# One more seven-product unit in the first down group of both FFNs, and the rotation tables and causal mask moved into a tile of the mixer

## The chip, the cores and the metric

The kernel runs on one core of a Trainium2 chip. Its time is the device time of one execution, in microseconds (us); several executions are timed and their median is compared. Five engines work side by side, each through its own list of instructions: PE (TensorE, the matmuls; PEld is its loading of weights), DVE (VectorE), ACT (ScalarE), POOL (GpSimd) and SP (SyncE, which only issues transfers here). They wait for each other by semaphores.

## The reference

One decoder layer on 256 rows of 2048 floats: a half-step SwiGLU FFN, a token mixer, a second FFN of the same kind, each added to the scaled stream and layer-normalised. Cut to what matters here:

```python
def swiglu(x, w_gate, w_up, w_down):            # w_gate, w_up: 2048 x 5632; w_down: 5632 x 2048
    return (jax.nn.silu(x @ w_gate) * (x @ w_up)) @ w_down
...
x = layer_norm(DEEPNORM_ALPHA * x + FFN_RES_WEIGHT * swiglu(x, ffn1_w_gate[l], ffn1_w_up[l], ffn1_w_down[l]), ...)
...
mix = jnp.concatenate([o_mla, o_nsa], axis=-1) @ w_out[l]     # the mixer: two attentions behind x @ w_in[l]
x = layer_norm(DEEPNORM_ALPHA * x + mix, ln2_g[l], ln2_b[l])
x = layer_norm(DEEPNORM_ALPHA * x + FFN_RES_WEIGHT * swiglu(x, ffn2_w_gate[l], ffn2_w_up[l], ffn2_w_down[l]), ...)
...
def rope(x, pos):                                          # the rotation: tables of cos and sin by position
    ...
    return jnp.concatenate([x1 * cos - x2 * sin, x2 * cos + x1 * sin], axis=-1)
```

Only the mixer uses the rotation tables and the causal mask.

## The kernel before

**Precision.** Everything is float32, done by split products. `split` writes `hi`, the value rounded to the matmul's type, on ACT (L95), and `lo`, what is left, on DVE (L96). `mm3` (L100 to L102) makes one product of three matmuls: hi by hi, hi by lo, lo by hi. Names in the profile: `raw` is a loaded weight tile, `whi` and `wlo` its parts; `thi` and `tlo` are the parts of the transposed activations; `sum` is a sum of weights; `m` is a 4 KB tile of the mixer's pool, of which there are `NM`.

**A stage of an FFN** (`gemm2`) computes two column chunks of 512 for both row tiles of 128. It goes through k in units of two k-tiles of 128. A plain unit has 8 products, so 24 matmuls of 128x512, and two weight tiles of 128x1024 to split. A unit in the list `seven` has 7 products, 21 matmuls, after the scheme of Strassen and Winograd: DVE adds weight tiles (L326 128x1024, L327 and L328 128x512), the sums are split too, and the products p1, p5, p6, p7 go into banks of their own. It also needs four sums of the activations (L405 to L408, 128x128), split into one `m` tile. After the last seven-product unit of a stage ACT copies p1 (L365) and DVE combines the four (L366 to L369); at the end of the stage four adds (L384) give the results. An up stage then multiplies by the gate (L516), a gate stage applies Silu on ACT (L494).

**The order of an FFN** is gate(0), up(0), gate(2), up(2), gate(4), down(0), up(4), gate(6), up(6), gate(8), up(8), the last pair `_gu`, down(1). The number is the first column chunk. The first down group, down(0), is called group one here: it multiplies what the first four chunks of the hidden layer give, eight units of k (0 to 7), into the columns of the output, first column pair cp 0, then cp 1. Both pairs take the order and the seven-product units of the table `DOWN, DOWN7`. The transposes of a hidden chunk (`trans`, L476) are spawned after its up stage and come into the next gate stage behind its last seven-product unit, at its tail: chunks 2 and 3 in gate(4)'s tail, chunks 4 and 5 in gate(6)'s... each chunk holds two units, so unit 4 is the first half of chunk 2. For a chunk with a unit in `SUMMED` the transposed bank is also copied to a `w` tile by ACT (L483), and L405 to L408 run on the copies; for the others there are only the split's cast (L485) and subtraction (L486). The banks of group one are seeded with the scaled residual by ACT (L544).

**What sets the order.** PE and SP run in the order of the program text; a small table of lanes (`tick`, `spawn`, `held`) interleaves the transposes there. On DVE, ACT and POOL a scheduler places the instructions when the program is built, and each engine then runs its list from top to bottom. Weight tiles come from rotating buffers: 5 for `raw`, 3 for `sum`, 6 each for `whi` and `wlo`.

**The constants.** `load_consts` loads 926 floats per partition into a tile `pack` in ffn1's first stage, 768 of them the rotation tables, and POOL builds the causal mask `cmask`. Both stay for the whole kernel.

Of the kernel before, what the change touches and what calls it, by code (L numbers as in the profile page):

```python
# [11 lines left out]
F32 = mybir.dt.float32  # L12
F32R = mybir.dt.float32r
AF = mybir.ActivationFunctionType
OP = mybir.AluOpType
# [3 lines left out]
P = 128  # L19
D = 2048  # L20
S = 256
NT = S // P
# [6 lines left out]
NEG = -1e30  # L29
# [4 lines left out]
O_CKV, O_KR, O_Q, O_KC, O_KS, O_KW, O_G = 512, 768, 832, 1856, 2368, 2880, 3392  # L34
KT = 2
HEAD, SPARE = 8, 2
NM = 8
NW = 9

GATE, GATE7 = (0, 1, 2, 3, 4, 5, 6, 7), (2, 4, 5)  # L40
UP, UP7 = (0, 1, 3, 2, 4, 6, 5, 7), (1, 2, 4, 5)
LATE = (0, 3, 1, 6, 2, 4, 5, 7)
DOWN, DOWN7 = (4, 0, 1, 5, 2, 3, 6, 7), (0, 1, 2, 3)
SUMMED = (0, 1, 2, 3, 8, 9, 10, 11, 18, 19, 20)
REST7 = ((8, 9, 10, 11, 18, 19, 20), (8, 9, 10, 11, 18, 19))
REST = ((12, 13, 14, 15, 8, 9, 16, 10, 11, 17, 18, 19, 20, 21), (12, 13, 8, 9, 14, 10, 11, 15, 18, 19, 16, 17, 20, 21))

# [6 lines left out]
def layer(ctx: ExitStack, tc: tile.TileContext, a: dict, out: bass.AP):  # L54
    nc = tc.nc
    PE, V, A, G = nc.tensor, nc.vector, nc.scalar, nc.gpsimd

    const = ctx.enter_context(tc.tile_pool(name="const", bufs=1))
# [17 lines left out]
    def am(dt=F32):  # L76
        return att.tile([P, 8, P], dt, name="m", bufs=NM)

# [35 lines left out]
    def spawn(gen, lane=None):  # L114

        lanes.setdefault(lane if lane is not None else object(), []).append([now[0], gen])
# [274 lines left out]
    def sl(pair, j):  # L391
        return pair[0][:, j, :], pair[1][:, j, :]
# [8 lines left out]
    def sums(v):  # L401

        x11, x12, x21, x22 = v
        s = wk([P, 4, P])
        V.tensor_tensor(s[:, 0], x21, x22, op=OP.subtract)  # L405
        V.tensor_tensor(s[:, 1], s[:, 0], x11, op=OP.subtract)
        V.tensor_tensor(s[:, 2], x11, x21, op=OP.subtract)
        V.tensor_tensor(s[:, 3], s[:, 1], x12, op=OP.add)  # L408
        return s

    def parts(s):
        hl = am2(F32R)
        split(*hl, s)
        return hl
# [3 lines left out]
    def load_x(k, n=2):  # L418
# [10 lines left out]
        if k // KT in UP7:  # L429
            xs0[k // KT] = parts(sums([raw[:, j, t * P:(t + 1) * P] for t in range(NT) for j in range(2)]))  # L430

    def load_consts():
        c = {}
        kept = sum(w for n, w in _PACK if n[:2] != "w2")
        pack = const.tile([P, kept], F32, name="pack")
        nc.sync.dma_start(pack, a["pack"][:, :kept])
        at = 0
        for n, w in _PACK:
            c[n] = (a["pack"] if n[:2] == "w2" else pack)[:, at:at + w]
            if n[:3] in ("cos", "sin"):  # L440
                c[n] = c[n].rearrange("p (t d) -> p t d", t=NT)
            at += w
        z = const.tile([P, S], F32, name="cmask")
        G.memset(z, 0.0)

        G.affine_select(out=z[:, P:], in_=z[:, P:], pattern=[[-1, P]], compare_op=OP.is_ge, fill=NEG, base=0,
                        channel_multiplier=1)
        c["mask"] = z
        one = const.tile([P, NT, NCMP], F32, name="vmask")
        G.memset(one, 1.0)  # L450
        zero = const.tile([P, NT, NCMP], F32, name="nmask")
        G.memset(zero, 0.0)
        for m, fill in ((one, 0.0), (zero, NEG)):
            G.affine_select(out=m, in_=m, pattern=[[P, NT], [-CS, NCMP]], compare_op=OP.is_ge, fill=fill,
                            base=-(CB - 1), channel_multiplier=1)
        c["valid"], c["neg"] = one, zero
        mh = const.tile([P, 1], F32, name="mhalf")
        G.memset(mh, -0.5)
        c["mhalf"] = mh
        return c  # L460


    def ffn(name, x, xs, done, begin=None, after=None, late=()):
# [3 lines left out]
        def trans(cs, ready, want=()):  # L467

            for c in cs:
                v, units = [], [i for i in range(KT) if 2 * c + i in want]  # L470
                while held[0] or now[0] < ready:
                    yield 1
                pts = [new_bank().rearrange("p (a b) -> p a b", a=4) for _ in range(NT)]
                for t in range(NT):
                    for j in range(4):
                        PE.matmul(pts[t][:, j, :], hs[c, t][:, j * P:(j + 1) * P], ident, start=j == 0, stop=j == 3,  # L476
                                  is_transpose=True, skip_group_check=True)
                for t in range(NT):
                    hT[c, t] = new_T()
                    src = pts[t]  # L480
                    if units:
                        src = wk([P, 4, P])
                        A.copy(src, pts[t])  # L483
                        v.append(src)
                    A.copy(hT[c, t][0], pts[t])  # L485
                    V.tensor_tensor(hT[c, t][1], src, f(hT[c, t][0]), op=OP.subtract)  # L486
                if units:
                    for i in units:
                        hS[2 * c + i] = parts(sums([u[:, KT * i + j] for u in v for j in range(KT)]))
                yield 2  # L490
# [22 lines left out]
        def up(c0):  # L513
# [5 lines left out]
            if c0 < 8:  # L519
                spawn(trans((c0, c0 + 1), now[0] + DFF, SUMMED), "T")  # L520

        def last():
# [8 lines left out]
            gemm2(x, xs, GATE, GATE7, name + "_gu", 0, fin)  # L531
            spawn(trans((8, 9, 10), now[0] + DLAST, SUMMED), "T")

        def down(gi):
            xh = lambda k, t: sl(hT[k // 4, t], k % 4)

            def rows(t, n):
                return y[t][:, n * NCH:(n + 1) * NCH]

            for cp in range(2):  # L540
                order, sevens = (REST[cp], REST7[cp]) if gi else (DOWN, DOWN7)
                gemm2(xh, hS, order, sevens, name + "_w_down", cp, lambda t, j, r: done(t, 2 * cp + j) if gi else None,
                      tail=3 if gi and cp else 0, into=lambda t, j: rows(t, 2 * cp + j),
                      seed=lambda t, j, b: A.activation(b, rows(t, 2 * cp + j), AF.Identity, scale=1.0 if gi else 2 * ALPHA))  # L544


        for step, n in ((gate, 0), (up, 0), (gate, 2), (up, 2), (gate, 4), (down, 0), (up, 4), (gate, 6), (up, 6), (gate, 8),
                        (up, 8)):
            step(n)
        last()  # L550
        down(1)


# [83 lines left out]
    cst = {}  # L637
# [475 lines left out]
def _rope_tables(d):  # L1113
# [7 lines left out]
_PACK = (("cos128", 256), ("sin128", 256), ("cos64", 128), ("sin64", 128), ("ln1_g", 16), ("ln1_b", 16), ("ln2_g", 16),  # L1121
         ("ln2_b", 16), ("nsa_gate_b", 24), ("mla_q_norm_g", 4), ("mla_kv_norm_g", 2), ("pe_k", 32), ("pe_v", 32), ("w2_k", 256), ("w2_v", 256))
# [69 lines left out]
```

## Time and profile before

| what | us |
|---|---|
| median of 3 runs | 1754.5 (1754.39 to 1756.76) |
| the profiled execution | 1758.64 |
| its span, first to last instruction | 1756.9 |
| PE busy (8040 matmuls) | 1736.7, 99% |
| DVE busy | 1586.5, 90% |
| ACT busy | 1023.5, 58% |
| POOL busy | 17.0, 1% |
| DMA queue of SP, share of 16 engines | 58.4% |

The profiled execution lies 4.1 us above the median, 1.7 us of which is outside the span. In ffn1 the stages that matter lie, by the trace, so (us from the start): gate(4) about 178 to 219.5, group one cp 0 219.5 to 260.3, cp 1 260.3 to 301.1, up(4) 301.1 to 341.9, gate(6) 341.9 to about 385, up(6) to 426, then gate(8). In ffn2 group one lies at 1267.2 to 1348.8 and up(6) ends at 1474. A view by stretches gives the busy time of each engine in a stretch and the granted clock; in a timeline a row gives start, duration, engine, line, operation and, in brackets, the idle time ahead of it with what ended it. Matmul durations overlap: the pitch from start to start is what counts.

### The profile page before, as it was taken

What the parts mean: (1) busy time and instruction counts of PE and PEld (TensorE: products, weight loads), DVE (VectorE), ACT (ScalarE), POOL (GpSimd) and SP (SyncE); (2) the same over time, 40 slices, a digit from 0 to 9 for tenths busy, and PEclk for the clock granted to TensorE, in tenths of its full rate; (3) what the DMA queues carried; (4) which work ended last, traced back from release to release, by engine and by line L of the source; (5) the groups of instructions that cost most, each with busy time, mean ns of one, the idle gap of its engine ahead of it and who ended that gap; (6) DMA issues with size and microseconds to landing.
All of it is one profiled execution on the core that took longest, in us unless ns stands there. A gap on an engine that the chain in (4) does not pass through costs nothing. (4 is left out here: it accounts for less than half of the span.)

```text
span 1756.9 us, 22430 instructions
## 1 busy us (share of the span) xinstructions
PE 1736.7 (99%) x8040; PEld 1428.9 (81%) x8040; DVE 1586.5 (90%) x2099; ACT 1023.5 (58%) x1354; POOL 17.0 (1%) x39
## 2 busy tenths in 40 slices
PE   9999999999999999999999999999999999999997
PEld 7888888888888887887788788888888888888886
DVE  7899999999999998865586679899999999999998
ACT  6656565565656665654365545665655565656652
POOL 0000000000000000000000001000000000000000
PEclk9999999999999999999999999999999999999999
DMA  9665656556666566546753345654656655665665
GB/s 337 218 216 172 212 198 215 185 188 200 212 206 220 168 203 232 178 159 213 260 193 131 120 169 175 216 196 168 215 192 215 205 195 200 206 201 192 204 203 180
DMA packets 100336, 350.01 MB, mean 199 GB/s; under 512 B 11136, under 2 KB 13696, under 8 KB 100224
## 3 DMA queue, kind: packets, MB, share of 16 engines
q1 hardware_dynamic: 98944, 344.39, 58.4%
q0 software_dynamic: 1280, 4.20, 0.9%
q8 instruction: 63, 1.03, 0.2%
q14 instruction: 49, 0.40, 0.1%
HBM read 346.44 MB, written 2.10 MB: 198 GB/s over the span
## 5 line engine op out<-in xcount | busy, mean ns | idle before, releaser
L100 PE MATMUL bank<-whi,thi 128*128 128x512 f32 (+1 forms) x1904 | 748.6, 393 | 1.5 <-ACT whi L95 1.5
L101 PE MATMUL bank<-wlo,thi 128*128 128x512 f32 (+1 forms) x1904 | 740.8, 389 | 3.2 <-DVE wlo L96 3.1
L102 PE MATMUL bank<-whi,tlo 128*128 128x512 f32 (+1 forms) x1904 | 740.0, 389 | 0.2 <-DVE tlo L96 0.2
L95 ACT CAST whi<-raw 128x1024 fp32r<-128x1024 f32 (+1 forms) x577 | 540.6, 962 | 270.5 <-PE bank L102 142.9
L96 DVE TENSOR_TENSOR wlo<-raw,whi 128x1024 fp32r<-128x1024 f32 (+1 forms) x577 | 631.6, 1109 | 61.0 <-ACT whi L95 60.1
L95 ACT CAST whi<-sum 128x1024 fp32r<-128x1024 f32 x271 | 282.5, 1050 | 337.8 <-DVE sum L328 124.3
L100 PEld LDWEIGHTS bank<-whi,thi 128*128 128x128 f32 x1904 | 357.9, 188 | 79.3 <-issue 4.1
L101 PEld LDWEIGHTS bank<-wlo,thi 128*128 128x128 f32 x1904 | 358.1, 188 | 77.5 <-DVE wlo L96 7.0
L102 PEld LDWEIGHTS bank<-whi,tlo 128*128 128x128 f32 x1904 | 357.8, 188 | 74.3 <-DVE tlo L96 0.6
L96 DVE TENSOR_TENSOR wlo<-sum,whi 128x1024 fp32r<-128x1024 f32 x271 | 324.9, 1216 | 32.4 <-ACT whi L95 29.9
L100 PE MATMUL bank<-whi,m 128*128 128x512 f32 x448 | 174.3, 389 | 0.0
L101 PE MATMUL bank<-wlo,m 128*128 128x512 f32 x448 | 174.3, 389 | 0.0
L102 PE MATMUL bank<-whi,m 128*128 128x512 f32 x448 | 174.3, 389 | 0.0
L326 DVE TENSOR_TENSOR sum<-raw 128x1024 f32<-128x1024 f32 x112 | 136.7, 1220 | 12.4 <-DMA raw<-in_ffn_w_up 10.5
L101 PEld LDWEIGHTS bank<-wlo,m 128*128 128x128 f32 x448 | 84.1, 188 | 17.5
L102 PEld LDWEIGHTS bank<-whi,m 128*128 128x128 f32 x448 | 84.1, 188 | 17.5
L100 PEld LDWEIGHTS bank<-whi,m 128*128 128x128 f32 x448 | 84.1, 188 | 17.5
L328 DVE TENSOR_TENSOR sum<-sum,raw 128x512 f32<-128x512 f32 x112 | 76.9, 686 | 0.2
L327 DVE TENSOR_TENSOR sum<-sum,raw 128x512 f32<-128x512 f32 x112 | 76.8, 686 | 0.1
L384 DVE TENSOR_TENSOR w<-bank,w 128x512 f32<-128x512 f32 x80 | 51.8, 683 | 2.2 <-PE bank L102 2.2
L777 ACT ACTIVATE w<-w,mx 128x256 f32<-128x256 f32 (+1 forms) x48 | 21.3, 445 | 27.5 <-DVE mx L773 24.6
L384 DVE TENSOR_TENSOR y<-bank,w 128x512 f32<-128x512 f32 x32 | 20.7, 683 | 6.8 <-PE bank L102 6.8
(187 smaller groups left out, 946.5 us busy)
## 6 DMA issues: line engine op xcount, KB each, us to landing
raw<-in_ffn_w_down SPq DMA_DIRECT2D x176, 512.0 KB, 4.5
raw<-in_ffn_w_up SPq DMA_DIRECT2D x160, 512.0 KB, 4.7
raw<-in_ffn_w_gate SPq DMA_DIRECT2D x146, 512.0 KB, 4.7
raw<-in_ffn_gu SPq DMA_DIRECT2D x32, 512.0 KB, 5.0
raw<-in_w_in SPq DMA_DIRECT2D x30, 512.0 KB, 5.2
raw<-in_w_out SPq DMA_DIRECT2D x20, 512.0 KB, 3.3
sum<-in_w_in SPq DMA_DIRECT2D x18, 512.0 KB, 5.3
sum<-in_ffn_w_gate SPq DMA_DIRECT2D x12, 512.0 KB, 4.8
```

The source lines that it names most:

```text
L95: A.copy(hi, src)
L96: V.tensor_tensor(lo, src, f(hi), op=OP.subtract)
L100: PE.matmul(ps, xh, wh, start=first and not onto, stop=False, skip_group_check=onto)
L101: PE.matmul(ps, xh, wl, start=False, stop=False, skip_group_check=onto)
L102: PE.matmul(ps, xl, wh, start=False, stop=last, skip_group_check=onto)
L326: V.tensor_tensor(t13, a_, b_[:, 1:2, :].broadcast_to([P, 2, NCH]), op=OP.add)
L327: V.tensor_tensor(t24[:, 0], t13[:, 0], a_[:, 1], op=OP.add)
L328: V.tensor_tensor(t24[:, 1], t24[:, 0], b_[:, 0], op=OP.add)
L384: V.tensor_tensor(r, B[b], rest[b], op=OP.add)
L777: A.activation(s[:, h, :], s[:, h, :], AF.Exp, bias=mx[:, h:h + 1], accum_out=sm[:, h:h + 1])
```

## The change

The table for group one now has one entry for each column pair. cp 0 keeps its order and its four seven-product units. cp 1 takes the units in the order 5, 0, 1, 6, 2, 3, 4, 7, and 0 to 4 are seven-product units: five, the last three of them in a row. Unit 4 joins `SUMMED`, so chunk 2's transposes get the two copies, the four sums and a split into one more `m` tile, in gate(4)'s tail of both FFNs. `NM` goes from 8 to 9. To make room, the rotation tables (768 floats per partition) and the mask leave the constants; after ffn1 a fresh `m` tile takes both, by one transfer and two POOL instructions.

```diff
--- before.py
+++ after.py
@@ -34,14 +34,14 @@
 O_CKV, O_KR, O_Q, O_KC, O_KS, O_KW, O_G = 512, 768, 832, 1856, 2368, 2880, 3392
 KT = 2
 HEAD, SPARE = 8, 2
-NM = 8
+NM = 9
 NW = 9
 
 GATE, GATE7 = (0, 1, 2, 3, 4, 5, 6, 7), (2, 4, 5)
 UP, UP7 = (0, 1, 3, 2, 4, 6, 5, 7), (1, 2, 4, 5)
 LATE = (0, 3, 1, 6, 2, 4, 5, 7)
-DOWN, DOWN7 = (4, 0, 1, 5, 2, 3, 6, 7), (0, 1, 2, 3)
-SUMMED = (0, 1, 2, 3, 8, 9, 10, 11, 18, 19, 20)
+DOWN, DOWN7 = ((4, 0, 1, 5, 2, 3, 6, 7), (5, 0, 1, 6, 2, 3, 4, 7)), ((0, 1, 2, 3), (0, 1, 2, 3, 4))
+SUMMED = (0, 1, 2, 3, 4, 8, 9, 10, 11, 18, 19, 20)
 REST7 = ((8, 9, 10, 11, 18, 19, 20), (8, 9, 10, 11, 18, 19))
 REST = ((12, 13, 14, 15, 8, 9, 16, 10, 11, 17, 18, 19, 20, 21), (12, 13, 8, 9, 14, 10, 11, 15, 18, 19, 16, 17, 20, 21))
 
@@ -429,23 +429,18 @@
         if k // KT in UP7:
             xs0[k // KT] = parts(sums([raw[:, j, t * P:(t + 1) * P] for t in range(NT) for j in range(2)]))
 
+    TAB = sum(w for n, w in _PACK if n[:3] in ("cos", "sin"))
+
     def load_consts():
         c = {}
-        kept = sum(w for n, w in _PACK if n[:2] != "w2")
+        kept = sum(w for n, w in _PACK if n[:2] != "w2") - TAB
         pack = const.tile([P, kept], F32, name="pack")
-        nc.sync.dma_start(pack, a["pack"][:, :kept])
+        nc.sync.dma_start(pack, a["pack"][:, TAB:TAB + kept])
         at = 0
         for n, w in _PACK:
-            c[n] = (a["pack"] if n[:2] == "w2" else pack)[:, at:at + w]
-            if n[:3] in ("cos", "sin"):
-                c[n] = c[n].rearrange("p (t d) -> p t d", t=NT)
+            if at >= TAB:
+                c[n] = a["pack"][:, at:at + w] if n[:2] == "w2" else pack[:, at - TAB:at - TAB + w]
             at += w
-        z = const.tile([P, S], F32, name="cmask")
-        G.memset(z, 0.0)
-
-        G.affine_select(out=z[:, P:], in_=z[:, P:], pattern=[[-1, P]], compare_op=OP.is_ge, fill=NEG, base=0,
-                        channel_multiplier=1)
-        c["mask"] = z
         one = const.tile([P, NT, NCMP], F32, name="vmask")
         G.memset(one, 1.0)
         zero = const.tile([P, NT, NCMP], F32, name="nmask")
@@ -538,7 +533,7 @@
                 return y[t][:, n * NCH:(n + 1) * NCH]
 
             for cp in range(2):
-                order, sevens = (REST[cp], REST7[cp]) if gi else (DOWN, DOWN7)
+                order, sevens = (REST[cp], REST7[cp]) if gi else (DOWN[cp], DOWN7[cp])
                 gemm2(xh, hS, order, sevens, name + "_w_down", cp, lambda t, j, r: done(t, 2 * cp + j) if gi else None,
                       tail=3 if gi and cp else 0, into=lambda t, j: rows(t, 2 * cp + j),
                       seed=lambda t, j, b: A.activation(b, rows(t, 2 * cp + j), AF.Identity, scale=1.0 if gi else 2 * ALPHA))
@@ -658,6 +653,20 @@
 
     ffn("ffn1", lambda k, t: sl(xT[k // 4, t], k % 4), xs0, done1, begin=begin, after=load_y)
 
+
+    tab = am().rearrange("p a b -> p (a b)")
+    nc.sync.dma_start(tab[:, :TAB], a["pack"][:, :TAB])
+    at = 0
+    for n, w in _PACK:
+        if at < TAB:
+            cst[n] = tab[:, at:at + w].rearrange("p (t d) -> p t d", t=NT)
+        at += w
+    z = tab[:, TAB:TAB + S]
+    G.memset(z, 0.0)
+
+    G.affine_select(out=z[:, P:], in_=z[:, P:], pattern=[[-1, P]], compare_op=OP.is_ge, fill=NEG, base=0,
+                    channel_multiplier=1)
+    cst["mask"] = z
 
     w_in = W["w_in"]
     xin = lambda k, t: sl(x1[k // 4, t], k % 4)
```

Line numbers shift with it: L483, L485, L486, L494, L516 and L544 of before are L478, L480, L481, L489, L511 and L539 of the changed kernel.

On PE six matmuls are gone in the whole program (7840 to 7834 rows of its list), three in each cp 1 of group one; nothing else moves there. On SP the early transfer of `pack` is 128x158 in place of 128x926, and a transfer `m<-in_pack 128x768` stands behind ffn1's last weight loads and ahead of the mixer's first. On POOL the mask's two instructions stand in the same place. DVE and ACT get the added instructions, and the scheduler orders them otherwise in both FFNs, from gate(4)'s tail to up(4) and again from gate(6)'s tail to gate(8); the mixer's order is the same.

First place: ACT in gate(4)'s tail and at the start of group one. `L365` is gate(4)'s copy of p1, `whi<-raw` are casts of weight tiles, `L485`/`L480` the casts of transposed chunks, `L544`/`L539` the seeds. Before:

```order
L365 COPY w<-bank 128x512
L95 CAST whi<-raw 128x1024 x5
L485 CAST thi<-bank 128x512 x2
L95 CAST whi<-raw 128x1024
L95 CAST whi<-raw 128x512
L95 CAST whi<-sum 128x1024
L485 CAST thi<-bank 128x512 x2
```

Now:

```order
L365 COPY w<-bank 128x512
L95 CAST whi<-raw 128x1024 x6
L478 COPY w<-bank 128x512
L480 CAST thi<-bank 128x512
L478 COPY w<-bank 128x512
L480 CAST thi<-bank 128x512
L95 CAST whi<-raw 128x512
L95 CAST m<-w 128x512
```

The sixth weight cast, which is that of group one's first seven-product unit, stood behind chunk 2's casts and now stands ahead of them and of the two new copies. On DVE one weight split and then chunk 2's `tlo` stand behind L369 in this place.

Second place: ACT in gate(6)'s tail, the transposes of chunks 4 and 5. Before:

```order
L365 COPY w<-bank 128x512
L95 CAST whi<-raw 128x1024 x5
L483 COPY w<-bank 128x512
L485 CAST thi<-bank 128x512
L483 COPY w<-bank 128x512
```

Now:

```order
L365 COPY w<-bank 128x512
L95 CAST whi<-raw 128x1024 x6
L478 COPY w<-bank 128x512
L480 CAST thi<-bank 128x512
L478 COPY w<-bank 128x512
```

Here too one weight cast more stands ahead of the copies.

Third place: DVE from up(6)'s last seven-product unit to gate(8). `wlo<-sum` are the two splits of the sums of that unit; the `wlo<-raw` behind them are the two tiles of up(6)'s last, plain unit and then gate(8)'s first tiles. Before:

```order
L96 TENSOR_TENSOR wlo<-sum,whi 128x1024 x2
L96 TENSOR_TENSOR wlo<-raw,whi 128x1024 x2
L366 TENSOR_TENSOR w<-bank,w 128x512
L96 TENSOR_TENSOR wlo<-raw,whi 128x1024
L367 TENSOR_TENSOR w<-bank,w 128x512
L96 TENSOR_TENSOR wlo<-raw,whi 128x1024
L368 TENSOR_TENSOR w<-bank,w 128x512
L369 TENSOR_TENSOR w<-bank,w 128x512
L384 TENSOR_TENSOR w<-bank,w 128x512 x2
L516 TENSOR_TENSOR w<-w 128x512 x2
L384 TENSOR_TENSOR w<-bank,w 128x512 x2
L516 TENSOR_TENSOR w<-w 128x512 x2
```

Now:

```order
L96 TENSOR_TENSOR wlo<-sum,whi 128x1024 x2
L96 TENSOR_TENSOR wlo<-raw,whi 128x1024
L366 TENSOR_TENSOR w<-bank,w 128x512
L96 TENSOR_TENSOR wlo<-raw,whi 128x1024
L367 TENSOR_TENSOR w<-bank,w 128x512
L96 TENSOR_TENSOR wlo<-raw,whi 128x1024
L368 TENSOR_TENSOR w<-bank,w 128x512
L369 TENSOR_TENSOR w<-bank,w 128x512
L384 TENSOR_TENSOR w<-bank,w 128x512 x2
L511 TENSOR_TENSOR w<-w 128x512 x2
L384 TENSOR_TENSOR w<-bank,w 128x512 x2
L511 TENSOR_TENSOR w<-w 128x512 x2
```

Before, four weight splits stand between the sums and the block of L384 and L516: both tiles of up(6)'s last unit and both of gate(8)'s first. Now there are three: the second tile of gate(8)'s first unit stands behind the block.

## The prediction

> **What bounds the kernel now.** I read the page's busy shares first, then the view by stretches over the FFNs, then timelines of DVE and PE at the tightest places, then the waits.
>
> ```profile
> PE 1736.7 (99%) x8040; PEld 1428.9 (81%) x8040; DVE 1586.5 (90%) x2099; ACT 1023.5 (58%) x1354; POOL 17.0 (1%) x39
> ...
> 301.10:341.90 40.80, 40.80 (x181) 33.78 (x180) 37.60 (x42) 23.47 (x25) 0.00 (x0) 1.00 0.60 198
> 170.00:426.00 256.00, 255.82 (x1146) 211.84 (x1145) 250.04 (x298) 155.18 (x182) 0.00 (x0) 1.00 0.61 203
> 1348.80:1389.60 40.80, 40.80 (x182) 33.78 (x181) 36.80 (x42) 23.33 (x25) 0.00 (x0) 1.00 0.57 191
> 1218.00:1474.00 256.00, 256.00 (x1147) 212.32 (x1146) 249.58 (x299) 154.41 (x182) 0.00 (x0) 1.00 0.60 203
> ```
>
> Columns from the second row on: the stretch, its length, busy time of PE, PEld, DVE, ACT, POOL, then the granted clock and DMA. PE is full, so matmuls removed should count at once. But from gate(4) to the end of up(6) DVE is nearly full too: 250.04 of 256 us in ffn1, so it idles 5.96 us, 3.2 of them in up(4) (301.10 to 341.90); in ffn2 6.4 and 4.0. So there are two bounds side by side, and the change takes from one and gives to the other. How little DVE is ahead shows at the end of up(6), whose last seven-product unit starts this timeline of DVE; the second fence is PE's.
>
> ```profile
> 412.24 1.24 DVE L326 TENSOR_TENSOR sum<-raw 128x1024 f32<-128x1024 f32 x1
> 413.38 1.24 DVE L96 TENSOR_TENSOR wlo<-raw,whi 128x1024 fp32r<-128x1024 f32 x1
> 414.51 0.71 DVE L327 TENSOR_TENSOR sum<-sum,raw 128x512 f32<-128x512 f32 x1
> 415.11 0.70 DVE L96 TENSOR_TENSOR wlo<-raw,whi 128x512 fp32r<-128x512 f32 x1
> 415.72 0.70 DVE L328 TENSOR_TENSOR sum<-sum,raw 128x512 f32<-128x512 f32 x1
> 416.32 2.53 DVE L96 TENSOR_TENSOR wlo<-sum,whi 128x1024 fp32r<-128x1024 f32 x2
> 419.05 2.36 DVE L96 TENSOR_TENSOR wlo<-raw,whi 128x1024 fp32r<-128x1024 f32 x2 [0.20 <-ACT whi L95]
> 421.33 0.68 DVE L366 TENSOR_TENSOR w<-bank,w 128x512 f32<-128x512 f32 x1
> ...
> 425.99 1.28 DVE L384 TENSOR_TENSOR w<-bank,w 128x512 f32<-128x512 f32 x2
> ...
> 430.79 2.35 DVE L96 TENSOR_TENSOR wlo<-raw,whi 128x1024 fp32r<-128x1024 f32 x2
> ```
>
> ```profile
> 418.05 0.39 PE L101 MATMUL bank<-wlo,m 128*128 128x512 f32 x1
> 418.28 0.39 PE L102 MATMUL bank<-whi,m 128*128 128x512 f32 x1
> ...
> 428.93 0.39 PE L101 MATMUL bank<-wlo,thi 128*128 128x512 f32 x1
> ...
> 431.43 0.39 PE L100 MATMUL bank<-whi,thi 128*128 128x512 f32 x1
> 432.06 0.50 PE L101 MATMUL bank<-wlo,thi 128*128 128x512 f32 x1 [0.25 <-DVE wlo L96]
> ```
>
> The first sum's `wlo` is done at 416.32 + 1.22 = 417.54 and PE uses it at 418.05: DVE is 0.51 us ahead. At 431.43 it is behind: PE's next start comes after 0.63 us in place of 0.23, so 0.40 us are lost. ffn2's last up(6) unit reads alike:
>
> ```profile
> 1463.69 2.50 DVE L96 TENSOR_TENSOR wlo<-sum,whi 128x1024 fp32r<-128x1024 f32 x2
> ...
> 1465.72 0.39 PE L101 MATMUL bank<-wlo,m 128*128 128x512 f32 x1
> ```
>
> Done at 1464.91, used at 1465.72: 0.81 us ahead.
>
> **The matmuls removed.** PE's pitch is 0.23 us (418.05 to 418.28; 0.227 over many). Three matmuls less in each FFN are 0.68 us, in both 1.36 us. This counts only where PE does not wait for DVE.
>
> **What DVE is given.** Pitches are differences of starts above: 1.14 for a 128x1024 (412.24 to 413.38), 0.60 for a 128x512 (414.51 to 415.11). A seven-product unit costs L326 1.14, split 1.14, L327 0.60, split 0.60, L328 0.60 and two splits of sums 2.28, together 6.36. A plain unit costs two splits, 2.28. So unit 4 costs 4.08 more. Its activations cost four sums and one split:
>
> ```profile
> 388.06 0.29 DVE L405 TENSOR_TENSOR w<-w 128x128 f32<-128x128 f32 x1
> 388.26 0.29 DVE L408 TENSOR_TENSOR w<-w 128x128 f32<-128x128 f32 x1
> ```
>
> 4 x 0.20 + 0.60 (a 128x512 as above) = 1.40. So DVE gets 5.5 us more work in each FFN, ahead of up(6), with 0.51 us (0.81) in hand at its end. In group one itself, the third seven-product unit in a row takes DVE 6.36 us where PE needs 21 x 0.227 = 4.77, so the lead that DVE has there shrinks by 1.6 us per unit and PE begins to wait in cp 1 already; where it waits matters less than how much of the 5.5 us DVE gets back before up(6) ends. What it can get back is its idle time:
>
> ```profile
> DVE sum L326 <- DMA raw<-in_ffn_w_up: 2.9, 3, 2.0
> DVE sum L326 <- DMA raw<-in_ffn_w_down: 0.8, 1, 0.8
> ```
>
> These waits (total, times, longest) between 170 and 440 us are 3.7 of the 5.96 us. Up(4)'s 3.2 us can be won, since a DVE that is late no longer runs ahead of its loads there. The bounds are thus: nothing won, and 3.2 (ffn1) won.
>
> **What the new order on ACT takes back.** Here the row by row reading of the changed lists comes in. In gate(4)'s tail the cast of group one's first unit now stands ahead of chunk 2's copies.
>
> ```profile
> 210.21 1.08 ACT L485 CAST thi<-bank 128x512 fp32r<-128x512 f32 x2
> 212.51 1.06 ACT L95 CAST whi<-raw 128x1024 fp32r<-128x1024 f32 x1 [1.22 <-DVE tlo L486]
> ...
> 210.58 0.68 DVE L369 TENSOR_TENSOR w<-bank,w 128x512 f32<-128x512 f32 x1
> ...
> 206.62 0.33 SPq L322 DMA_DIRECT2D raw<-in_ffn_w_down  x1
> ...
> raw<-in_ffn_w_down SPq DMA_DIRECT2D x1, 512.0 KB, 5.8
> ```
>
> That cast's weights are issued at 206.62 and land 5.8 us later, at 212.4; the cast starts at 212.51 and not sooner. Before, the transposed chunk's casts were done by then (from 210.21). Now the copy starts at 212.5 + 0.95 = 213.4, its `thi` at 213.9, and DVE's `tlo` can start at 214.5. DVE, with one weight split behind L369, is free at 210.58 + 0.60 + 1.14 = 212.3: it idles 2.2 us. The second place is gate(6)'s tail:
>
> ```profile
> 374.81 1.05 ACT L95 CAST whi<-raw 128x1024 fp32r<-128x1024 f32 x1 [2.39 <-DMA raw<-in_ffn_w_up]
> 376.17 1.05 ACT L95 CAST whi<-raw 128x1024 fp32r<-128x1024 f32 x1 [0.31 <-DMA raw<-in_ffn_w_up]
> 377.12 0.58 ACT L483 COPY w<-bank 128x512 f32<-128x512 f32 x1
> ```
>
> The casts ahead of the copies wait for their loads, 1.36 us apart; with one cast more the copies come at least one such step later, and DVE, again with one weight split in hand, waits for them: I put 1.4 to 2 us. Between cp 0 and cp 1 the 0.8 us for the load of w_down stays and may double, as its buffer is freed by DVE itself. So 2.2 + 1.4 to 2 + 0.8 to 2 = 4.4 to 6.2 us of idle time stand in the new order, against 5.96 in the old: what up(4) gives back, the tails take. Of the difference, -0.2 to 1.6, I take 0.5 us won in each FFN, below its middle, as the new order will have small waits that I do not count. DVE is then 5.5 - 0.5 = 5.0 us later at up(6)'s last seven-product unit, and PE 5.0 - 0.51 = 4.5 us (ffn1) and 5.0 - 0.81 = 4.2 us (ffn2). The matmuls saved are in this already: PE would be there earlier and waits for the same DVE. Bounds: 5.0 and 4.7 with nothing won; with up(4)'s idle won in full 5.5 - 3.2 - 0.51 = 1.8 and, with 4.0 us in ffn2, 0.7.
>
> **Gate(8)'s first unit.** The order of the third place decides it. PE stands at the last unit's first sum (the 418.05 row), waiting for `wlo`. From its end DVE has to do, in the new order: the second sum's split, three splits, L366 to L369, four L384, four L516, and then the second tile of gate(8)'s first unit: 4 x 1.14 + 4 x 0.60 + 8 x 0.60 + 1.22 = 13.0 us (the block alone is 425.99 to 430.79, 4.80). PE comes to that tile 428.93 - 418.05 = 10.9 us after the first sum. It waits 13.0 - 10.9 = 2.1 us. In the old order this tile is split ahead of the block, and the tile behind it waits only 0.40; with PE 2.1 later that wait is gone, 0.40 counted once, for ffn1. If DVE kept its old lead of 0.51 or 0.81 the wait would be 1.6 or 1.3: these are the lower bounds. In both FFNs: 2 x 2.1 - 0.4 = +3.8 (bounds 2.5 to 3.8).
>
> **The tables and the mask.** The transfer is 128 x 768 x 4 bytes, 0.39 MB, at the mixer's start, ahead of w_in's loads.
>
> ```profile
> 677.00:698.00 21.00, 19.32 (x76) 14.98 (x75) 15.53 (x23) 7.27 (x11) 0.55 (x1) 0.92 0.87 305
> ...
> 694.39 0.69 DVE L384 TENSOR_TENSOR y<-bank,w 128x512 f32<-128x512 f32 x1 [2.91 <-PE bank L102]
> 697.23 1.52 ACT L608 ACTIVATE y<-y,mr,rstd 128x512 f32<-128x512 f32 x2 [8.05 <-DVE mr L603]
> ```
>
> At 305 GB/s it takes 1.3 us and the DMA engines are 0.87 busy, so w_in's first tiles land up to 1.3 us later. Their splits lie ahead of DVE's wait of 2.91 us and ACT's of 8.05, which hide it. I take 0; without that cover it costs 1.3. The tile's last reader was done in `_gu`, so SP does not stop at it, and nothing behind it queues. POOL's two instructions lie beside a POOL that is busy 1%. The lighter first transfer frees time where PE is not waiting for it: 0.
>
> **Sum.** 4.5 + 4.2 + 3.8 = +12.5 us. The profiled execution would go from 1758.64 to 1771.1; it lies 4.1 above the median, so the median goes from 1754.5 to about 1767.
>
> **Rivals.**
> (a) As above: 1767, its own range 1763 to 1770. Chance 0.60.
> (b) Up(4)'s idle time is won in full, so the tails' new idle costs nothing: 1.8 + 0.7 + 3.8 = +6.3, so 1761. For it: a load's wait shifts with DVE; against it: 212.4 is a landing, not DVE's doing. Chance 0.18.
> (c) Not slower: DVE's lead covers all. It would need DVE over 2.1 us ahead at up(6)'s last seven-product unit in spite of 5.5 us more work; then PE's six matmuls count, -1.36, so 1753.1. It decides from the point where the lead at 418.05 falls under 2.1 us; the trace has 0.51 there with less work. For it speaks only that DVE may wait less on ACT and loads than the old rows show. Chance 0.10.
> (d) The clock falls after a wait.
>
> ```profile
> 685.00:688.40 3.40, 1.72 (x6) 0.91 (x6) 1.80 (x4) 2.55 (x4) 0.00 (x0) 1.00 0.77 275
> 688.40:691.80 3.40, 3.40 (x10) 2.62 (x9) 3.08 (x6) 0.78 (x2) 0.00 (x0) 0.50 0.98 363
> ```
>
> After 3.4 us in which PE was busy 1.72, the granted clock was 0.50 for 3.4 us, which costs 1.7. A wait of 2.1 us at gate(8) leaves PE busy 1.3 of 3.4 us if it falls into one such stretch whole, more if into two, so the clock may fall in each FFN: 1767 + 2 x 1.7 = 1770.4. The Trainium skill ("TensorE: Matmul & The Clock Gate", "The HAM clock gate") has the clock fall after a whole idle window of about 3.4 us; by that rule waits of 2.1 us cost nothing more and the time stays at 1767. The trace's drop came after a stretch only half idle, so the rule does not exclude it. Chance 0.08.
> (e) The tables' transfer delays ffn1's last weights or the mixer's first, 1.3 us on top: 1768.3. Chance 0.04.
>
> **How the numbers follow.** (a), (b), (d), (e) are slower and hold 0.90; I leave some of it to the tail of (b) under 3.5 us. A change under 0.2%, 3.5 us, cannot be told from none here. Faster needs -3.5 us, more than double what PE can save: 0.03, for what I have not seen. Same 0.12, slower 0.85. The range from 1757.5 to 1772 takes in (b) and (d) and leaves out (c).
>
> **What would show it.** Right: 7840 to 7834 matmuls; PE waits on `wlo` (L96) at the last two seven-product units of cp 1, in up(6)'s sevens, and about 2 us at gate(8)'s first unit; DVE idle about 2 us ahead of `tlo` in gate(4)'s tail; nothing new in the mixer. Wrong: up(6) without waits, or DVE's idle time from 170 to 426 falling well under 5 us; then (b) or (c). A granted clock under 1.0 behind gate(8)'s wait would be (d), a later w_in landing with PE waiting (e).

## The result and the profile after

The changed kernel takes 1768.6 us (median of 4 runs, 1767.65 to 1770.18); the kernel before takes 1755.6 beside it (4 runs, 1754.39 to 1756.76). The ratio is 1.0072, 95% interval 1.006 to 1.0084: slower by 13 us. The forecast was 1767, +12.5; 1.1 us of the 1.6 between 1767 and 1768.6 is the starting point, 1754.5 in the forecast and 1755.6 beside the changed kernel.

The page of the changed kernel: its first part, and the two groups of PE with the longest idle time (the last columns: busy time and mean, then idle time ahead and what ended it). The last row is the first of these groups in the kernel before; the second had no idle time there:

```profile
PE 1740.1 (98%) x8034; PEld 1426.3 (81%) x8034; DVE 1598.4 (90%) x2119; ACT 1027.2 (58%) x1364; POOL 17.4 (1%) x39
...
L101 PE MATMUL bank<-wlo,thi 128*128 128x512 f32 (+1 forms) x1894 | 737.5, 389 | 7.4 <-DVE wlo L96 7.4
...
L101 PE MATMUL bank<-wlo,m 128*128 128x512 f32 x456 | 178.7, 392 | 2.8 <-DVE wlo L96 2.8
...
L101 PE MATMUL bank<-wlo,thi 128*128 128x512 f32 (+1 forms) x1904 | 740.8, 389 | 3.2 <-DVE wlo L96 3.1
```

PE has six matmuls less (8040 to 8034) and DVE 11.9 us more work (1586.5 to 1598.4). Before, L101 idled 3.2 us in the whole kernel, 3.1 of it for `wlo`; now it is 7.4 + 2.8.

The same stretches of ffn1 as in the prediction, shifted by what PE is late there (gate(4) to the end of up(6), and up(4)):

```profile
170.00:430.80 260.80, 258.01 (x1144) 210.66 (x1143) 254.69 (x308) 156.27 (x187) 0.00 (x0) 1.00 0.60 198
301.80:342.60 40.80, 40.80 (x181) 33.78 (x181) 40.40 (x45) 23.81 (x26) 0.00 (x0) 1.00 0.64 215
```

DVE idles 260.80 - 254.69 = 6.11 us, against 5.96 before. In up(4) its idle time fell from 3.2 to 0.4. So up(4) gave back 2.8 us, and as much arose elsewhere. Where, the timelines show: ACT and DVE in gate(4)'s tail, DVE between group one's pairs, and DVE in gate(6)'s tail. The last row is the kernel before, where chunk 2's `tlo` in gate(4)'s tail had no wait.

```profile
212.26 1.05 ACT L95 CAST whi<-raw 128x1024 fp32r<-128x1024 f32 x1 [2.23 <-DMA raw<-in_ffn_w_down]
213.21 0.58 ACT L478 COPY w<-bank 128x512 f32<-128x512 f32 x1
...
210.82 1.21 DVE L96 TENSOR_TENSOR wlo<-raw,whi 128x1024 fp32r<-128x1024 f32 x1
214.31 0.69 DVE L481 TENSOR_TENSOR tlo<-w,thi 128x512 fp32r<-128x512 f32 x1 [2.27 <-ACT thi L480]
...
260.41 1.23 DVE L326 TENSOR_TENSOR sum<-raw 128x1024 f32<-128x1024 f32 x1 [1.65 <-DMA raw<-in_ffn_w_down]
...
382.06 0.69 DVE L481 TENSOR_TENSOR tlo<-w,thi 128x512 fp32r<-128x512 f32 x1 [1.22 <-ACT thi L480]
...
211.18 1.28 DVE L486 TENSOR_TENSOR tlo<-bank,thi 128x512 fp32r<-128x512 f32 x2
```

ACT's cast waits 2.23 us for its weights with the copies queued behind it, and DVE waits 2.27 us for the first copy and the cast behind it. PE pays first at a place that the prediction does not name, the start of group one: its banks are seeded by ACT (L539), and on ACT the seeds now stand behind the cast of the sums, which waits for DVE's late sums (L408).

```profile
217.58 0.62 ACT L95 CAST m<-w 128x512 fp32r<-128x512 f32 x1 [1.81 <-DVE w L408]
...
221.72 0.50 PE L100 MATMUL bank<-whi,thi 128*128 128x512 f32 x1 [0.50 <-ACT bank L539]
```

By the same matmuls in both traces PE loses 1.2 us there in ffn1 and 1.0 in ffn2, and 0.6 and 0.5 more for a `wlo` at the first seven-product unit behind it. Then it pays where DVE's lead runs out. On PE: cp 1's last seven-product unit (two waits), up(6)'s last one, and gate(8)'s first unit, of ffn1 (upper six rows) and of ffn2 (the rest):

```profile
292.87 0.50 PE L101 MATMUL bank<-wlo,thi 128*128 128x512 f32 x1 [0.38 <-DVE wlo L96]
...
295.82 0.50 PE L101 MATMUL bank<-wlo,m 128*128 128x512 f32 x1 [0.59 <-DVE wlo L96]
...
421.72 0.39 PE L100 MATMUL bank<-whi,m 128*128 128x512 f32 x1
422.71 0.50 PE L101 MATMUL bank<-wlo,m 128*128 128x512 f32 x1 [0.61 <-DVE wlo L96]
...
433.50 0.39 PE L100 MATMUL bank<-whi,thi 128*128 128x512 f32 x1
435.77 0.50 PE L101 MATMUL bank<-wlo,thi 128*128 128x512 f32 x1 [1.89 <-DVE wlo L96]
...
1472.26 0.50 PE L101 MATMUL bank<-wlo,m 128*128 128x512 f32 x1 [0.59 <-DVE wlo L96]
...
1483.05 0.39 PE L100 MATMUL bank<-whi,thi 128*128 128x512 f32 x1
1485.33 0.50 PE L101 MATMUL bank<-wlo,thi 128*128 128x512 f32 x1 [1.89 <-DVE wlo L96]
```

At gate(8) the starts lie 2.27 and 2.28 us apart in place of 0.23: PE loses 2.05 us in both FFNs. Behind ffn2's, the granted clock fell, from 1486.28 to 1489.69 us. The stretches below are that one and others that lie whole steps of 3.413 us from it:

```profile
431.57:434.98 3.41, 2.31 (x11) 1.58 (x9) 3.41 (x7) 1.37 (x2) 0.00 (x0) 1.00 0.24 96
434.98:438.39 3.41, 2.62 (x11) 2.16 (x12) 3.41 (x4) 0.00 (x0) 0.00 (x0) 1.00 0.45 156
1482.87:1486.28 3.41, 1.52 (x7) 0.96 (x6) 3.41 (x5) 0.62 (x1) 0.00 (x0) 1.00 0.00 0
1486.28:1489.69 3.41, 3.41 (x10) 2.67 (x9) 3.41 (x4) 0.90 (x1) 0.00 (x0) 0.50 0.91 288
```

At half clock eight matmuls start 0.43 us apart in place of 0.23, which costs 1.6 us. The equal wait of ffn1 lies across the border of two such stretches, and the clock stayed at 1.00.

The profiled execution's span went from 1756.9 to 1768.5, +11.6. Following the same matmuls in both traces, ffn1 adds 6.2 us and ffn2 7.3, some 1.6 of that by the half clock, and about 1 falls at the end; 3.5 go the other way at the mixer's start, where the execution before had its two waits and half clock (685.00 to 691.80 in the prediction's rows) and this one has 0.33 us. That last is a difference between executions and no gain of the change: e1 has it too, with unchanged FFNs, and its median did not move, and in the traces of e2 and e11, where the tables stand in the same place, PE waits 1.03 us there.

The mean granted clock of an execution, to three digits, tells how often the clock fell: of the thirteen traces here, those without a low stretch ahead of the kernel's end have 0.998, those with one of 3.41 us have 0.997, and e10's, with five times 3.41 us, 0.993. The four executions of the changed kernel have 0.997 (1770.18 us, the profiled one), 0.998 (1767.65), 0.996 (1768.35) and 0.998 (1768.9). So two of them had no low stretch and are still 12 and 13 us slower than the kernel before: the loss is not the clock's.

### The profile page after: what moved, and what is told of

Its sections match the earlier page's. It is cut to its first block, busy times and chain, and to the rows that moved or that the text cites. A ratio compares the mean times of both kernels' runs of the same rounds, so it can differ in the third digit from the quotient of the medians.

```text
span 1768.5 us, 22459 instructions
## 1 busy us (share of the span) xinstructions
PE 1740.1 (98%) x8034; PEld 1426.3 (81%) x8034; DVE 1598.4 (90%) x2119; ACT 1027.2 (58%) x1364; POOL 17.4 (1%) x39
## 3 DMA queue, kind: packets, MB, share of 16 engines
q8 instruction: 63, 1.03, 0.2%
## 5 line engine op out<-in xcount | busy, mean ns | idle before, releaser
L101 PE MATMUL bank<-wlo,thi 128*128 128x512 f32 (+1 forms) x1894 | 737.5, 389 | 7.4 <-DVE wlo L96 7.4
L95 ACT CAST whi<-sum 128x1024 fp32r<-128x1024 f32 (+1 forms) x275 | 286.4, 1049 | 358.0 <-DVE sum L328 144.9
L101 PEld LDWEIGHTS bank<-wlo,thi 128*128 128x128 f32 x1894 | 356.3, 188 | 82.9 <-DVE wlo L96 13.0
L96 DVE TENSOR_TENSOR wlo<-sum,whi 128x1024 fp32r<-128x1024 f32 (+1 forms) x275 | 329.5, 1213 | 35.6 <-ACT whi L95 31.9
L101 PE MATMUL bank<-wlo,m 128*128 128x512 f32 x456 | 178.7, 392 | 2.8 <-DVE wlo L96 2.8
L102 PE MATMUL bank<-whi,m 128*128 128x512 f32 x456 | 177.5, 389 | 0.0
L100 PE MATMUL bank<-whi,m 128*128 128x512 f32 x456 | 177.5, 389 | 0.0
L101 PEld LDWEIGHTS bank<-wlo,m 128*128 128x128 f32 x456 | 85.6, 188 | 24.5 <-DVE wlo L96 6.9
L384 DVE TENSOR_TENSOR w<-bank,w 128x512 f32<-128x512 f32 x80 | 51.6, 680 | 1.5 <-PE bank L102 1.5
L95 ACT CAST m<-w 128x512 fp32r<-128x512 f32 x32 | 19.6, 621 | 13.2 <-DVE w L408 13.2
```

Source lines behind the costliest of these rows:

```text
L95: A.copy(hi, src)
L96: V.tensor_tensor(lo, src, f(hi), op=OP.subtract)
L100: PE.matmul(ps, xh, wh, start=first and not onto, stop=False, skip_group_check=onto)
L101: PE.matmul(ps, xh, wl, start=False, stop=False, skip_group_check=onto)
L102: PE.matmul(ps, xl, wh, start=False, stop=last, skip_group_check=onto)
L384: V.tensor_tensor(r, B[b], rest[b], op=OP.add)
```

## The experiments

Each is timed against the kernel before on the same chip; gains in us are differences of ratios times 1755.5. Source lines in the profiles of e3 to e11 can be shifted by the edits; the operations tell which is which.

**e1: the tables alone.**

```diff
-DOWN, DOWN7 = ((4, 0, 1, 5, 2, 3, 6, 7), (5, 0, 1, 6, 2, 3, 4, 7)), ((0, 1, 2, 3), (0, 1, 2, 3, 4))
-SUMMED = (0, 1, 2, 3, 4, 8, 9, 10, 11, 18, 19, 20)
+DOWN, DOWN7 = ((4, 0, 1, 5, 2, 3, 6, 7),) * 2, ((0, 1, 2, 3),) * 2
+SUMMED = (0, 1, 2, 3, 8, 9, 10, 11, 18, 19, 20)
```

> Only the move of the tables and the mask into an m tile behind ffn1, with nine m tiles; group one keeps four seven-product units in both pairs and unit 4 has no sums. Theory A (DVE is given 5.5 us per FFN that it cannot make up, and the new orders on ACT and DVE add waits): nothing changes, 1755.5 within 1.5 us, and no new wait at the mixer's start. Rival B (the tables' transfer delays the mixer's first tiles, or the moved tile its users): up to 1.3 us for the transfer, 1757 or more; if the whole loss sat here, 1768.

Measured: ratio 1.0002 (0.9994 to 1.0011). The move of the tables and the mask costs nothing that can be measured. Rival B falls.

**e2: unit 4's activation sums without its seven products.** Only the `DOWN` line of e1's diff.

> As e1, and unit 4 is in SUMMED: chunk 2's copies, four sums and the split into an m tile are made in gate(4)'s tail, but no product uses them. Theory A: DVE gets 1.4 us and some 2.2 us of idle time in gate(4)'s tail per FFN; PE waits only at the start of group one, about 1.6 to 1.8 us per FFN, and up(4)'s idle time of 3.2 and 4.0 us takes up the rest ahead of up(6): +3.5, 1759. If work on DVE had no price, 1755.5.

Measured: ratio 1.002 (1.0011 to 1.0029), 1760.4 beside 1756.6: +3.5 us at the price of the ratio, as expected of theory A. So a quarter of the loss comes with 1.4 us of added sums per FFN and the order that they bring on ACT, with PE's list as before. In its trace PE waits at the start of group one alone, 1.65 us in ffn1 and 1.75 in ffn2, first for the seeds as above.

**e3: the seven products without their weight sums.**

```diff
-            if i in seven:
+            bare = "down" in w and i == 4 and i in seven
+            if i in seven and not bare:
                 t13, t24 = (sump.tile([P, KT, NCH], F32, name="sum") for _ in range(2))
 ...
+            if bare:
+                wt.update(t1=wt["kn"], t2=wt["kn"], t3=wt["lm"], t4=wt["lm"])
```

> The changed kernel, but unit 4's seven products use the parts of the raw tile where the weight sums t1 to t4 belong: L326 to L328 and the two splits of sums are left out for that unit, so its product is not the reference's; PE's list is the same length as the changed kernel's. DVE does 1.14 + 0.60 us for this unit in place of 6.36. Theory A: the waits of cp 1's last units are gone, those of group one's start (1.6 us per FFN, as in e2) stay, a little is left at gate(8): 1755.5 + 4 = 1759 to 1760. Rival C (the products themselves, the banks or PE's own order cost the time): 1768.6 as in the changed kernel. If only the weight sums mattered: 1755.5 - 1.4 = 1754.

Measured: ratio 1.0019 (1.0011 to 1.0027), +3.3 us. PE's list is that of the changed kernel, so the products, their banks and their order are not what costs the time: rival C falls. Some 10 us of the 13 hang on the weight sums, 4.6 us of DVE work per FFN. But they do not hang on the work alone, for without the sums the scheduler does not make two of the three new orders. ACT has six weight casts ahead of the copies in gate(4)'s tail, as in the changed kernel, but five in gate(6)'s, as before; and on DVE four weight splits stand ahead of the block at up(6)'s end (L387 here), with gate(8)'s second tile among them:

```profile
422.17 2.36 DVE L96 TENSOR_TENSOR wlo<-raw,whi 128x1024 fp32r<-128x1024 f32 x2 [0.21 <-PE bank L102]
...
425.05 1.22 DVE L96 TENSOR_TENSOR wlo<-raw,whi 128x1024 fp32r<-128x1024 f32 x1
...
426.78 1.22 DVE L96 TENSOR_TENSOR wlo<-raw,whi 128x1024 fp32r<-128x1024 f32 x1
...
429.11 1.28 DVE L387 TENSOR_TENSOR w<-bank,w 128x512 f32<-128x512 f32 x2
```

**e4: one seven-product unit less in up(6).**

```diff
-            gemm2(x, xs, LATE if c0 in (2, 4, 6) else UP, UP7, name + "_w_up", ...
+            gemm2(x, xs, LATE if c0 in (2, 4, 6) else UP, UP7[:3] if c0 == 6 else UP7, name + "_w_up", ...
```

> The changed kernel with up(6) on three seven-product units in place of four (units 1, 2, 4; unit 5 plain) in both FFNs: PE gets six matmuls more (1.4 us), DVE 4.1 us less per FFN, behind group one and ahead of gate(8). Theory A: the waits of up(6)'s sevens (about 1.6 us per FFN) and of gate(8)'s first unit (2.05 us) go, those of group one stay: 1768.6 - 2 x 3.65 + 1.4 = 1762.7. If PE were the bound in up(6): 1768.6 + 1.4 = 1770.

Measured: 1763.6, ratio 1.0039 (1.0027 to 1.0051) to before; 5.8 us less loss than the changed kernel, with six matmuls more. In its trace PE waits at most 0.3 us at a time in up(6) and at gate(8). What relieves DVE pays, even where it costs PE; but in this list, too, gate(8)'s second tile stands ahead of the block, so part of the gain is the order that e6 tests.

**e5: the copies of the transposes first, on ACT.** An order edge without a semaphore.

```diff
+                    last_copy = A.copy(hT[c, t][0], pts[t])
 ...
+                if c in (2, 4):
+                    behind[:] = [[last_copy, 0]]
 ...
-                split(hi[:, :n], lw[:, :n], v[:, :n])
+                c, _ = split(hi[:, :n], lw[:, :n], v[:, :n])
+                if behind:
+                    behind[0][1] += 1
+                    if behind[0][1] > 2:
+                        order_after(c, behind.pop(0)[0])
```

> The changed kernel with one order edge on ACT in each of the tails of gate(4) and gate(6), in both FFNs: the third weight cast behind the transposes of chunks 2 and 4 may not stand ahead of their last copy. No work is added or taken. Theory A: DVE's 2.2 us of idle time in gate(4)'s tail and 1.2 in gate(6)'s go, but not all of it reaches PE, as the waits of cp 1's last seven-product units (0.7 and 0.9 us) and gate(8)'s 2.05 have their own cause: about 4 us of the 13 are won, 1764.5. If ACT's order did not matter: 1768.6. If it were the whole cause: 1755.

Measured: 1766.0, ratio 1.006 (1.0046 to 1.0074): 2.1 us less loss than the changed kernel by the two ratios, whose intervals overlap. In its trace the idle time of gate(4)'s tail is gone. DVE's `tlo` there:

```profile
211.06 0.69 DVE L490 TENSOR_TENSOR tlo<-w,thi 128x512 fp32r<-128x512 f32 x1 [0.20 <-ACT thi L489]
```

0.20 us in place of 2.27. With it PE's wait for the seeds at the start of group one is gone in ffn1 and down to 0.39 us in ffn2. The gain on the whole is smaller than the 4 us expected. Its profiled execution (mean clock 0.997) has one low stretch, behind gate(8)'s wait in ffn1; the other four have 0.995 to 0.997, by the scale above one to three low stretches each, against none to two in the changed kernel. At 1.6 us each that can make up the missing 2 us.

**e6: gate(8)'s second tile ahead of the block, on DVE.**

```diff
+                fin = V.tensor_tensor(r, B[b], rest[b], op=OP.add)
+                if lead and b == OUT[0]:
+                    ahead_of.append(fin)
 ...
+                _, d = split(hi[:, :n], lw[:, :n], v[:, :n])
+                if ahead_of:
+                    ahead_of.append(d)
+                    if len(ahead_of) == 3:
+                        order_after(ahead_of[0], ahead_of[2])
 ...
```

`lead` is set for the up(6) stage.

> The changed kernel with one order edge on DVE per FFN: the block of L384 and L511 at up(6)'s end stands behind the split of gate(8)'s first unit's second tile, as in the kernel before. Theory A: PE's wait of 2.05 us there falls to about 0.45 (the tile behind it is then late, as before), 1.6 us per FFN: 1768.6 - 3.2 = 1765.4. Rival: the wait moves on in full, since DVE is late anyway: 1768.6.

Measured: 1765.1, ratio 1.0053 (1.004 to 1.0066): 3.3 us less by the ratios, as expected, though the intervals overlap a little. In its trace the wait at gate(8) is 0.38 us, at the tile behind, as in the kernel before.

**e7: both edges.**

> e5 and e6 together. Theory A: the two gains add, 4 + 3.2 us: 1768.6 - 7 = 1761.5; what is left over 1755.5 is DVE's added work of 5.5 us per FFN that nothing hides, mostly at cp 1's third seven-product unit in a row. If both edges only shift the same wait: 1764.5.

Measured: 1760.7, ratio 1.0027 (1.0018 to 1.0037). So 8 us of the 13 are won without taking any work away, where the two gains expected were 4 and 3.2. Each edge shows beside the other: e7 is 5.8 us better than e5 and 4.6 better than e6, and its interval overlaps neither of theirs. That both together win more than the 2.1 and 3.3 us that they won singly is within the intervals. Its worst waits on PE in ffn1 are 0.64 us in cp 1, 0.77 in up(6) and 0.35 at gate(8), where the clock stays at 1.00.

**e8: the multiplications on POOL.**

```diff
-                V.tensor_tensor(hs[c0 + j, t], r, sg[c0 + j, t], op=OP.mult)
+                G.tensor_tensor(hs[c0 + j, t], r, sg[c0 + j, t], op=OP.mult)
```

> The changed kernel with the up stages' multiplications by the gate (L511, 40 of 128x512) on POOL in place of DVE, 2.4 us per up stage taken from DVE. Theory A, if POOL's work costs DVE nothing: DVE is no longer the bound ahead of gate(8), the waits go, and the matmuls saved count: 1755.5 - 1.4 = 1754. Rival: POOL's instructions hold up DVE's, as the Trainium skill has it (SBUF - State Buffer: a DVE operation with two inputs in SBUF and a GpSimd operation that reads SBUF exclude each other for the whole instruction); then DVE loses the length of each multiplication on POOL, and if that is longer than the 0.60 us it took on DVE nothing is won: 1768 or more. DVE's splits near L511 would show durations over 1.22 us.

Measured: 1766.3, ratio 1.0057 (1.0045 to 1.007). Taking 2.4 us per up stage from DVE wins 2.6 us in all by the ratios, whose intervals overlap, and not 14. POOL and DVE behind up(6), and DVE's groups from 170 to 440 us:

```profile
430.29 7.01 POOL L511 TENSOR_TENSOR w<-w 128x512 f32<-128x512 f32 x4 [79.32 <-DVE w L384]
...
431.83 4.32 DVE L96 TENSOR_TENSOR wlo<-raw,whi 128x1024 fp32r<-128x1024 f32 x2
436.08 2.30 DVE L326 TENSOR_TENSOR sum<-raw 128x1024 f32<-128x1024 f32 x1
438.30 1.21 DVE L96 TENSOR_TENSOR wlo<-raw,whi 128x1024 fp32r<-128x1024 f32 x1
...
L96 DVE TENSOR_TENSOR wlo<-raw,whi 128x1024 fp32r<-128x1024 f32 x79 | 100.5, 1290 | 1.2 <-ACT whi L95 1.1
...
L326 DVE TENSOR_TENSOR sum<-raw 128x1024 f32<-128x1024 f32 x24 | 32.5, 1353 | 1.5 <-DMA raw<-in_ffn_w_down 1.1 <-DMA raw<-in_ffn_w_gate 0.2
```

Each multiplication takes 1.75 us on POOL, and while the four run, DVE's 128x1024 operations take 2.2 to 2.3 us in place of 1.22. Three of them take 6.5 us here, from 431.83 to 438.30, in place of 3.4: DVE loses some 3 us behind this up stage to win 2.4. The rule of the Trainium skill that the expectation names agrees in direction; by this trace DVE did not stand still for the whole 7 us, as three of its operations went through beside POOL's four.

**e9: both edges and no weight sums.** e7's and e3's edits in one kernel.

> e7 (both order edges) and e3 (unit 4's weight sums and their splits left out, so its product is not the reference's) in one kernel. Theory A: what e7 still loses is DVE's added work; with most of it gone the waits of cp 1's third seven-product unit go too, 0.8 us at group one's start and 0.5 to 0.7 at up(6) and gate(8) remain per FFN: 1755.7 + 2, 1758. If the rest of e7's loss had nothing to do with DVE's work: 1760.7 as e7.

Measured: 1758.3, ratio 1.0019 (1.001 to 1.0028), +3.3 us; e3 without the edges had the same ratio. So no gain of the edges can be measured once the weight sums are gone. For gate(8) that had to be so: e3's list has its second tile ahead of the block already. Only ACT's edge is new here, and it wins nothing that shows, against 4.6 us with the weight sums (e6 to e7). The other way round, with both edges in place the weight sums cost 1.4 us (e9 to e7, whose intervals overlap). So the prices do not simply add: without any change of the work the orders account for 8 of the 13 us (e7). The lists of these kernels differ in other places too, so how much of this is DVE's lead and how much further order is not shown. Of the 3.3 us that are left, PE's waits in the trace are 1.15 and 0.48 us at group one's start, 0.77 in both up(6) stages and 0.4 at gate(8).

**e10: DVE's work alone.**

```diff
-                V.tensor_tensor(t13, a_, b_[:, 1:2, :].broadcast_to([P, 2, NCH]), op=OP.add)
+                for _ in range(5 if "down" in w and cp == 1 and i == 3 else 1):
+                    V.tensor_tensor(t13, a_, b_[:, 1:2, :].broadcast_to([P, 2, NCH]), op=OP.add)
```

> e1 (the tables' move alone, four seven-product units, PE's list as before) with DVE made to compute unit 3's first weight sum (L326) five times in cp 1 of group one: 4 x 1.14 = 4.6 us more DVE work per FFN in the place where unit 4's stood, with no change on PE, in the activations' sums or in ACT's tails. Theory A: the lead DVE has there (some 2.3 us) hides half, PE waits 2.3 us once per FFN, up(4)'s idle time hides the rest and neither up(6) nor gate(8) waits: 1756 + 4.6 = 1760.5. If DVE's work were all lost to PE: 1756 + 9.2 = 1765. If DVE's work did not count: 1756.

The edit stands on e1's tables. Measured: 1763.6 (1762.3 to 1769.1), ratio 1.0046 (1.0032 to 1.0059): +8.1 us, not 4.6. PE at the place, then three stretches of 3.4 us:

```profile
287.00 0.39 PE L102 MATMUL bank<-whi,tlo 128*128 128x512 f32 x1
289.80 0.50 PE L100 MATMUL bank<-whi,m 128*128 128x512 f32 x1 [2.41 <-ACT whi L95]
291.25 0.79 PE L101 MATMUL bank<-wlo,m 128*128 128x512 f32 x1 [0.95 <-DVE wlo L96]
...
286.90:290.30 3.40, 0.99 (x4) 0.25 (x2) 3.30 (x5) 1.20 (x2) 0.00 (x0) 1.00 0.00 0
290.30:293.70 3.40, 2.45 (x6) 1.97 (x7) 3.26 (x3) 3.40 (x4) 0.00 (x0) 0.50 0.76 259
293.70:297.10 3.40, 3.40 (x10) 2.63 (x9) 2.04 (x3) 2.32 (x3) 0.00 (x0) 0.50 0.55 196
```

PE waits 2.6 and 1.2 us in a row, first for ACT's cast of the sum and then for DVE's split of it, where 2.3 together were expected; in ffn2 it is 2.1 and 1.2. The lead is shorter than the expectation takes it to be: in e1's trace the split of that first sum starts at 285.32, is done 1.22 later, at 286.54, and PE uses it at 287.82, so 1.28 us are in hand and not 2.3, and 4.6 - 1.3 = 3.3 us must be waited for; the trace has 3.8 and 3.3. In this execution the clock then stands at 0.50 for 6.8 us in both FFNs, but it is the slowest of the five (1769.1, mean clock 0.993); the others have 0.996 and 0.997. So the waits, 7.1 us in the two FFNs, are most of the median's 8.1, and the clock is not. Nothing is late at up(6) or gate(8): up(4) hides the rest, as expected.

**e11: half of it.** Three times in place of five.

> e10 with two more L326 in place of four: 2.3 us of DVE work per FFN. Theory A with the clock: DVE's lead of some 2.3 us in cp 1 hides nearly all of it, PE waits 0.5 to 0.7 us once per FFN, too short for the granted clock to fall, and e10's excess over its expectation (8.7 in place of 4.6 us) came from the half clock behind its long waits: 1755 + 1.2 = 1756. If DVE's work cost PE in proportion, half of e10's loss: 1759.3.

Measured: 1760.3, ratio 1.0021 (1.0012 to 1.003), +3.7 us: nearer to proportion than to theory A with the clock. In its trace PE waits once per FFN in cp 1, 1.0 us each, which is what a lead of 1.28 leaves of 2.3 us, and the clock stays at 1.00; in ffn2 another 1.1 us fall at up(6) and gate(8), which e1's profiled execution has too without the added work. So about 2 of its 3.7 us are the added work by the trace; the other part is open.

No variant beats both kernels. The best with five seven-product units and all their sums, e7, is still 0.27% slower than the kernel before, and all that the six matmuls can save is 1.4 us.

## Why the prediction was right

The time, the sign and most places were forecast; the terms, one by one:

- **The matmuls removed** (1.36 us that do not count): 8040 to 8034 by the page (the forecast's 7840 and 7834 are another count, with the same six between them), and no part of it in the time. e4 agrees: six more matmuls with less DVE work are faster.
- **What DVE is given** (5.5 us per FFN, 11.0): 11.9 by the page. e3 shows that PE's new products cost nothing; e7 shows that 8 of the 13 us come from the orders that the scheduler gives this work, and not from its amount.
- **The idle time** (4.4 to 6.2 us in the new order against 5.96, of which 0.5 won): 6.11, so 0.15 lost. Gate(4)'s tail 2.27 (forecast 2.2), gate(6)'s 1.22 (1.4 to 2), the load between the pairs 1.65 (0.8 to 2), up(4)'s 3.2 down to 0.4. The balance was right within 0.7; the size of gate(6)'s term was off.
- **PE late at up(6)'s last seven-product unit** (4.5 and 4.2 us): in ffn1 the row at 418.05 is now at 422.71, 4.7 later, and this execution was some 0.3 us ahead of the other before gate(4)'s tail, so 5.0; in ffn2, counted from where ffn2's group one starts, 3.6. The sum of the two is 8.6 where 8.7 was forecast; that it fits so well is luck, as the terms are off by +0.5 and -0.6. On the way there the prediction missed a place: 1.8 and 1.5 us of this lateness arise at group one's start, two thirds of it behind ACT's seeds, and in cp 1 PE waits in the last seven-product unit only, not in the last two.
- **Gate(8)'s first unit** (2.1 us of wait): 2.05 in both, and e6 wins what this term says, 3.3 us. This one order, read from the list of instructions, was a quarter of the loss. With the wait of 0.40 that is gone in ffn1 the term is 3.7 in the trace without the half clock, where 3.8 was forecast.
- **The tables and the mask** (0): e1, 1.0002.
- **Rival (d), the clock**, was given 0.08 as a case of its own. It is not a rival but a part that comes and goes: behind the same wait of 2.05 us the clock fell in ffn2 and not in ffn1 of one execution. The prediction's reason, that it depends on whether the wait falls into one stretch whole, fits the rows above. It is worth 1.6 us where it falls. By the mean clocks one execution of the changed kernel had one low stretch, one had two and two had none, so it moves single executions and not the loss.
- **Rival (b)**, that up(4) gives its idle time back: it did, 2.8 of 3.2 us, and the tails took as much, which was the step that set (a) against (b). e5 and e7 confirm that the tails' part was an effect of the order and not of the work.

What the prediction does not say is that its terms depend on each other. It books DVE's 5.5 us of work as lost once up(4)'s gain is taken by the tails. With ACT's and DVE's orders mended the same work costs 4.7 us in both FFNs together (e7), 3.3 of them also without the weight sums (e9), and without the weight sums the scheduler itself leaves two of the three orders as they were (e3). Its sum holds for the lists that it read, and for no others.

## What to carry to other kernels

When an engine that is nearly full (here DVE, 250 of 256 us) feeds the bound one, a trade that gives it 5.5 us to save the other 0.7 is paid from the feeder's lead; read that lead at its thinnest place (here 0.51 us), and for the operand that comes last (e10), not the busy shares of the page. A scheduler's new order can cost as much as the work that caused it, so look in each engine's list for an instruction that waits for a load ahead of short ones that others wait for, and for a long block ahead of the next tile. Two order edges gave back 8 of 13 us here. And compare the lists of a variant before its time is read: a variant meant to take away work (e3, e4) had other orders too.

## What the runs showed of the hardware

The granted clock fell to 0.50 behind waits shorter than the stretch for which it then stays low. Low stretches of one execution begin whole steps of 3.413 us apart: e10's begin at 290.28, 710.12 and 1341.58 us, 123 and 185 steps. Counted so in the changed kernel's trace, a wait of 2.05 us that lies whole in one step, with PE busy 1.52 of 3.41 us, was followed by a step at half clock in ffn2; an equal wait across a border, with PE busy 2.31 and 2.62, was not, in ffn1. In e10 waits of 2.6 and 1.2 us were followed by two steps, 6.8 us, at half clock. The Trainium skill ("TensorE: Matmul & The Clock Gate", "The HAM clock gate") puts the drop behind an idle window of about 3.4 us; the length of the low stretch agrees with such a window, and the condition is weaker here than a window wholly idle: PE was busy for 1.52 us of it. Where the limit lies these runs do not show.

A multiplication of 128x512 with both inputs in SBUF takes 1.75 us on POOL against a pitch of 0.60 on DVE, and beside them a DVE operation of 1.22 us takes up to 2.3 (e8): behind up(6), work moved from DVE to POOL cost DVE some 3 us and saved it 2.4.
